# A two-layer hybrid block at full matmul occupancy: one weight sum moved to an accumulating transfer, sums and splits regrouped, two more seven-product groups

## The chip, the cores and the metric

The kernel runs on one core of one Trainium2 chip. The metric is the device time of one execution in microseconds; the median of three runs is given, with the lowest and the highest. A profile of one more execution gives its own time and, inside it, the span from the first to the last instruction.

The engines are called by the profile's names: PE (TensorE, matmuls), PEld (its weight loads), DVE (VectorE), ACT (ScalarE), POOL (GpSimd), SP (SyncE, which here only issues transfers).

## The reference

The input is one sequence of 256 rows with 2048 features in float32. Two layers are applied, and a last normalisation:

```
for layer in range(2):
    h = h + mixer(rmsnorm(h, norm[layer]))      # layer 0: gated delta rule + RG-LRU; layer 1: forgetting attention + block attention
    h = h + swiglu(rmsnorm(h, ffn_norm[layer]), w_gate, w_up, w_down)
return rmsnorm(h, final_norm)

swiglu(hn) = (silu(hn @ w_gate) * (hn @ w_up)) @ w_down      # 2048 -> 5632 -> 2048
```

Nearly all of the work is products of the 256 rows with weight matrices that are read once from memory. The two feed-forward parts (FFN, `swiglu`) take more than half of the time, and nearly all of the change lies there.

## The kernel before

**Exact products from two halves.** Every float32 matrix, weights and activations, is split into a high part in the matmul's reduced format (`hi`, a cast on ACT) and the remainder (`lo`, a subtraction on DVE). A product is three matmuls: high by high, high by low, low by high. A weight piece is 128 x 1024 (two tiles of 128 x 512, 512 KB). `load` (line 166) asks for it on SP's queue into a `raw` buffer; `split` (line 176) makes `whi` and `wlo`. One call of `Bank.add` (line 399) is one product of a piece with one half of the rows: two tiles by three matmuls of 128 x 512, six in all.

**Groups by sevens.** An FFN is cut into blocks (`block`, line 409). A gate-and-up block works out 512 columns of both the gate and the up matrix from all 2048 features; there are 11 in an FFN. Feature blocks are taken in groups of 512 features: for one group, the weights are a 2 by 2 matrix of pieces (`b11`, `b12`, `b21`, `b22`), and the rows of the activations are two halves. A plain group takes 8 products. A group by sevens (`seven`, line 424) takes 7, after Winograd's scheme: four of the seven use sums of the weight pieces, worked out on the fly, and three of them use combinations of the activations, which `combine` (line 382) works out once for a group of features and keeps in `comb`. Four of the products go to four banks `M[0]` to `M[3]` of their own, three right into the banks `F`; at the end of a block `ends` (line 449) takes the four together on ACT and DVE.

**Which groups are by sevens.** `groups` in `ffn` (line 501) gives for each of the 11 gate-and-up blocks how many of its four groups are done by sevens: none in block 0, two in every other. A piece of 4, 4 and 3 blocks is followed by two blocks of the down projection (`dn`), each with one group by sevens. That makes 26 groups by sevens per FFN.

**The sums before.** `total` (line 372) adds two pieces on DVE into a new tile `T`, and at once casts and splits the sum into `thi` and `tlo`. A group has four: T1 = `b11 + b12`, T3 = `b12 + b22`, T2 = T1 + `b22`, T4 = T2 + `b21`. The tag `T` has three buffers, which `combine` (its `cf` and `cc4`) and the scratch of the squares (`sumsq`, line 313) use as well.

**What sets the order.** The program is written in one order, and the framework's planner orders the instructions of each engine by priority in that order and by estimated times; semaphores follow from the tiles. Groups by sevens are generators of seven steps that are taken between the plain pieces: after piece `j` of a block, steps are taken up to `(j - lead + 2) * steps // gaps`, with `lead` plain pieces ahead and `trail` behind (line 475). `hooks` run before a plain piece: `turn` (the transposes of the last block's result) before piece 2, `rstd` and two `combine` in block 0, and the `combine` for the down projection (`late`) before piece 4 of one block.

**Buffers for weight pieces.** In the FFNs `load` takes three buffers of `wr` and four of `raw4`, four of each seven loads going to `raw4`; SP issues a load when the buffer is free again, so a buffer that is kept long holds up SP's queue. `whi` has four buffers, `wlo` three, `thi` and `tlo` two each.

**Start and end.** `first` (line 210) does the first four weight tiles while activations and weights come in, in 16 slices of features: four loads of one slice, then six of two; splits go by halves for the first two pairs (`u < 2`). In the LRU part of the first mixer every tile has a generator that runs beside the next tile's matmuls; `start(..., pace)` says after how many turns it takes its next step. At the end, `second_half` (line 1137) has a written order for DVE and ACT: last sums, squares, the root and reciprocal of the mean (`root`, `rate`), and the scaled outputs (`ready`).

Of the kernel before, what the change touches and what calls it, by code (L numbers as in the profile page):

```python
# [6 lines left out]
ALU = mybir.AluOpType  # L7
# [3 lines left out]
D = 2048  # L11
# [36 lines left out]
def body(tc, A, out):  # L48
# [117 lines left out]
    def load(src):  # L166

        loads[0] += 1
        if more and loads[0] > 0 and loads[0] % 7 in (1, 3, 5, 6):
            raw = mx.tile([128, 1024], F32, name="raw4", tag="raw4", bufs=4)  # L170
        else:
            raw = wr.tile([128, 1024], F32, name="raw")
        nc.sync.dma_start(raw, src)
        return raw
# [35 lines left out]
    def first(src, n, w):  # L210
# [7 lines left out]
        Ps = [acc.tile([128, T], F32, name="Pw", tag="acc") for _ in range(n)]  # L218
        for a, b in [(k, k + 1) for k in range(4)] + [(k, k + 2) for k in range(4, NK, 2)]:
            nc.sync.dma_start(xw[a // 4][:, a % 4:a % 4 + b - a], src[:, a:b])  # L220
            if b == 12:
                nc.sync.dma_start(tab[:, 0:NTAB0], A["tab"][:, 0:NTAB0])
                nc.sync.dma_start(col[:, 16:], A["col"][:, 16:])
        for u in range(NK // 2):
            hi = wh.tile([128, 1024], F32R, name="whi")
            lo = wl.tile([128, 1024], F32R, name="wlo")
            for a, b in [(0, 1), (1, 2)] if u < 2 else [(0, 2)]:
                ks = range(2 * u + a, 2 * u + b)
# [84 lines left out]
    def sumsq(g, *ts):  # L313
        for t in ts or range(2):
            j = (mx.tile([128, 1024], F32, name="junk", tag="T", bufs=3)[:, 0:512] if more else
                 mx.tile([128, 512], F32, name="junk", tag="t2", bufs=4))
            S.activation(j, h[:, t, g * 512:(g + 1) * 512], AF.Square, accum_out=ssp[:, t, g:g + 1])
# [53 lines left out]

    def total(a, b, name):

        t = mx.tile([128, 1024], F32, name=name, tag="T", bufs=3)
        V.tensor_tensor(out=t, in0=a, in1=b, op=ALU.add)  # L375
        hi = fp.tile([128, 1024], F32R, name="thi", tag="thi", bufs=2)
        lo = fp.tile([128, 1024], F32R, name="tlo", tag="tlo", bufs=2)
        S.copy(hi, t)  # L378
        V.tensor_sub(lo, t, hi.bitcast(F32))  # L379
        return t, (hi, lo)  # L380

    def combine(x4):

        f = mx.tile([128, 4, T], F32, name="cf", tag="T", bufs=3)
        c = mx.tile([128, 4, 2, 128], F32, name="cc4", tag="T", bufs=3)
        r = fp.tile([128, 2, 4, 2, 128], F32R, name="comb", tag="comb", bufs=3)
# [22 lines left out]
    def block(src, x, comb, nd, hooks, tail=0, lead=2, trail=None):  # L409
# [14 lines left out]
        def seven(m):  # L424
            c = comb[m]()
            cx = lambda i: lambda kk: [c[:, j, i, kk] for j in range(2)]
            q = lambda j, t: lambda kk: xs(4 * m + 2 * j + kk, t)
            b11 = load(src(0, 2 * m))
            M[0].add(q(0, 0), split(b11))
            yield  # L430
            b12 = load(src(1, 2 * m))
            t, w = total(b11, b12, "T1")
            M[1].add(cx(0), w)
            yield
            b22 = load(src(1, 2 * m + 1))
            F[0][1].add(cx(3), split(b22))
            yield
            M[3].add(cx(1), total(b12, b22, "T3")[1])
            yield
            t, w = total(t, b22, "T2")  # L440
            M[2].add(cx(2), w)
            yield
            b21 = load(src(0, 2 * m + 1))
            F[0][0].add(q(1, 0), split(b21))
            yield
            F[1][0].add(q(1, 1), total(t, b21, "T4")[1])
            yield
# [34 lines left out]
    def ffn(L, then, fin=None):  # L482
# [17 lines left out]

        for groups in ((0, 2, 2, 2), (2, 2, 2, 2), (2, 2, 2)):
            piece = len(groups)
            hid = ogp.tile([128, 16, 2, T], F32R, name="hid", tag="hid")
            late = {4: lambda hid=hid: ch.update({0: combine(hid[:, 0:4])})}
            for j in range(piece):
# [5 lines left out]
                if j == 1 and piece == 3:  # L511
                    hooks.update(late)
                F, e = block(lambda i, u: gu[b, u, i], lambda k: X[:, k], {m: lambda m=m: cx[m] for m in range(groups[j])}, 4, hooks)
                a = [fp.tile([128, 512], F32, name=f"fa{t}", tag="fa", bufs=2) for t in range(2)]
# [81 lines left out]
    def mixer0():  # L596
# [540 lines left out]
    def second_half(add):  # L1137

        o = fo[0]
        x, y, z = ([f[:, t:t + 1] for t in range(2)] for f in (xf, yf, zf))  # L1140

        def root(t):

            for i, o in ((2, z[t]), (3, x[t])):
                V.scalar_tensor_tensor(out=o, in0=ssp[:, t, i:i + 1], scalar=1.0 / D, in1=part[:, t:t + 1] if i == 2 else z[t],
                                       op0=ALU.mult, op1=ALU.add)
            S.activation(y[t], ssp[:, t, 3:4], AF.Sqrt, scale=1.0 / D, bias=z[t])
# [30 lines left out]
        rate(1)  # L1178
# [98 lines left out]
```

## Time and profile before

| what | value |
|---|---|
| median of 3 runs | 2233.04 us (2232.82 to 2233.43) |
| the profiled execution | 2232.51 us |
| its span, first to last instruction | 2230.7 us |
| granted PE clock | 0.999 |
| moved by transfers | 422.29 MB, mean 189 GB/s |
| first mixer, second mixer (about) | 0 to 433 us, 1101 to 1528 us |
| the two FFNs (about) | 433 to 1128 us, 1528 to 2221 us |

A row of a group names the line, the engine, the operation, output<-inputs by the program's names, the shape, the count, then the busy time, the mean time of one in ns, and the engine's idle time just before such an instruction with what ended it. A row of waits reads: who waited <- for whom: us in total, times, longest. A row of the timeline gives start and duration in us, and in brackets the idle time before it and what ended that. Matmuls overlap, so that their durations are longer than the distance between their starts.

### The profile page before, as it was taken

To read this page: it belongs to the slowest core of one execution; us is meant where nothing else is said; L and a number is where in the kernel's file an instruction comes from. 1 tells how busy PE (TensorE), PEld (TensorE's weight loads), DVE (VectorE), ACT (ScalarE), POOL (GpSimd) and SP (SyncE) were. 2 spreads that over 40 slices of the span, in tenths; PEclk is the share of its full clock that TensorE was granted. 3 is DMA by queue.
4 is the path that set the end of the run, shared out by engine and by line. 5 is a ranking of instruction groups with operands and counts; after the bars stand their busy time and mean duration, and the time that the engine had idled before them with its cause. 6 is when DMAs were issued, how large, how long until landed. Compare 5 with 4: busy or idle time off the path is not lost.

```text
span 2230.7 us, 30096 instructions
## 1 busy us (share of the span) xinstructions
PE 2215.9 (99%) x11026; PEld 1852.0 (83%) x11026; DVE 1928.9 (86%) x2716; ACT 1278.9 (57%) x1670; POOL 2.1 (0%) x6
## 2 busy tenths in 40 slices
PE   9999999999999999999999999999999999999998
PEld 8888888888888888888878888888888888888886
DVE  8899676789989999899966658857999999999998
ACT  6776664565555665565654444445665466555565
POOL 0000000000000000000000000000000000000000
PEclk9999999999999999999999999999999999999999
DMA  7445445665565666656545455456665666666563
GB/s 280 161 144 168 140 150 187 214 208 195 192 215 196 201 195 203 207 187 200 180 158 175 158 172 172 162 186 217 208 198 191 208 205 203 194 210 202 181 219 131
DMA packets 117780, 422.29 MB, mean 189 GB/s; under 512 B 13152, under 2 KB 14688, under 8 KB 117504
## 3 DMA queue, kind: packets, MB, share of 16 engines
q1 hardware_dynamic: 117344, 420.10, 56.7%
q8 instruction: 86, 1.41, 0.2%
q14 instruction: 62, 0.51, 0.1%
q10 hardware_dynamic: 288, 0.27, 0.0%
HBM read 418.22 MB, written 2.10 MB: 188 GB/s over the span
## 4 chain that ended last, share of the span: by engine, by line
PE 97%; DVE 1%; DMA 1%; ACT 0%; issue 0%; SPq 0%; DVEq 0%; ACTq 0%
PE F L405 16%; PE F L406 16%; PE F L404 16%; PE Pw L199 11%; PE Pw L204 6%; PE Px L303 5%; PE Px L305 5%; PE Px L304 5%; PE M L404 4%; PE M L405 4%; PE M L406 4%; PE Ph L492 1%; PE Psc L1053 1%; PE Pt L326 0%; PE Ps L563 0%; DMA raw<-in_gu 0%
## 5 line engine op out<-in xcount | busy, mean ns | idle before, releaser
L179 ACT CAST whi<-raw 128x1024 fp32r<-128x1024 f32 x724 | 760.7, 1052 | 744.8 <-PE F L406 359.1
L180 DVE TENSOR_TENSOR wlo<-raw,whi 128x1024 fp32r<-128x1024 f32 x724 | 876.5, 1219 | 185.0 <-PE Px L304 74.0
L199 PE MATMUL Pw<-X,whi 128*128 128x512 f32 x1088 | 388.0, 400 | 0.0
L404 PE MATMUL F<-whi,X 128*128 128x512 f32 x848 | 330.5, 391 | 0.0
L405 PE MATMUL F<-wlo,X 128*128 128x512 f32 x848 | 330.4, 390 | 0.0
L406 PE MATMUL F<-whi,X 128*128 128x512 f32 x848 | 330.1, 389 | 0.0
L204 PE MATMUL Pw<-X,wlo 128*128 128x256 f32 x1088 | 304.7, 280 | 0.1
L378 ACT CAST thi<-T 128x1024 fp32r<-128x1024 f32 x208 | 219.1, 1054 | 98.6 <-DVE T L375 71.5
L379 DVE TENSOR_TENSOR tlo<-T,thi 128x1024 fp32r<-128x1024 f32 x208 | 252.5, 1219 | 24.7 <-ACT thi L378 24.2
L199 PEld LDWEIGHTS Pw<-X,whi 128*128 128x128 f32 x1088 | 204.1, 188 | 47.4 <-issue 0.5
L405 PE MATMUL F<-wlo,hid 128*128 128x512 f32 x536 | 208.9, 390 | 0.0
L406 PE MATMUL F<-whi,hid 128*128 128x512 f32 x536 | 208.7, 389 | 0.0
L404 PE MATMUL F<-whi,hid 128*128 128x512 f32 x536 | 208.6, 390 | 0.0
L204 PEld LDWEIGHTS Pw<-X,wlo 128*128 128x128 f32 x1088 | 205.4, 189 | 1.2 <-DVE wlo L180 0.7
L406 PEld LDWEIGHTS F<-whi,X 128*128 128x128 f32 x848 | 159.2, 188 | 33.1
L404 PEld LDWEIGHTS F<-whi,X 128*128 128x128 f32 x848 | 159.2, 188 | 32.7
L405 PEld LDWEIGHTS F<-wlo,X 128*128 128x128 f32 x848 | 159.3, 188 | 32.5
L375 DVE TENSOR_TENSOR T<-raw,raw 128x1024 f32<-128x1024 f32 x98 | 119.2, 1218 | 11.0 <-DMA raw<-in_gu 8.9
L375 DVE TENSOR_TENSOR T<-T,raw 128x1024 f32<-128x1024 f32 x104 | 126.6, 1218 | 1.9 <-DMA raw<-in_dn 1.7
L404 PE MATMUL M<-thi,comb 128*128 128x512 f32 x312 | 121.3, 391 | 0.6 <-ACT thi L378 0.6
L405 PE MATMUL M<-tlo,comb 128*128 128x512 f32 x312 | 121.6, 390 | 0.0
L406 PE MATMUL M<-thi,comb 128*128 128x512 f32 x312 | 121.5, 389 | 0.0
(385 smaller groups left out, 3217.1 us busy)
## 6 DMA issues: line engine op xcount, KB each, us to landing
raw<-in_gu SPq DMA_DIRECT2D x352, 512.0 KB, 4.1
raw<-in_dn SPq DMA_DIRECT2D x176, 512.0 KB, 4.3
raw<-in_w0w SPq DMA_DIRECT2D x72, 512.0 KB, 3.6
raw<-in_wo SPq DMA_DIRECT2D x64, 512.0 KB, 3.5
raw<-in_w1w SPq DMA_DIRECT2D x64, 512.0 KB, 3.6
raw<-in_w1x SPq DMA_DIRECT2D x32, 512.0 KB, 3.6
raw<-in_w0x SPq DMA_DIRECT2D x16, 512.0 KB, 3.6
xw<-in_xw SPq DMA_DIRECT2D x6, 768.0 KB, 10.9
```

Of the source, the lines that this page charges most:

```text
L179: S.copy(hi, raw)
L180: V.tensor_sub(lo, raw, hi.bitcast(F32))
L199: PE.matmul(P.rearrange("p a b -> p (a b)"), hi[:, kk], X[:, k].rearrange("p a b -> p (a b)"), start=k == 0, stop=False)
L204: PE.matmul(P[:, 0], lo[:, kk], X[:, k, 0], start=False, stop=k == NK - 1)
L303: PE.matmul(Ps[t], x[:, 0, ts], hi[:, kk], start=k == 0, stop=False)
L304: PE.matmul(Ps[t], x[:, 0, ts], lo[:, kk], start=False, stop=False)
L375: V.tensor_tensor(out=t, in0=a, in1=b, op=ALU.add)
L378: S.copy(hi, t)
L379: V.tensor_sub(lo, t, hi.bitcast(F32))
L404: PE.matmul(self.t, xh, hi[:, kk], start=self.i == kk == 0, stop=False)
L405: PE.matmul(self.t, xh, lo[:, kk], start=False, stop=False)
L406: PE.matmul(self.t, xl, hi[:, kk], start=False, stop=kk == 1 and self.i == self.n - 1)
```

## The change

- In a group by sevens, only three sums stay on DVE. The first, `b11 + b12`, is written to `T`; the later ones are added to the same tile in place, each after the split of the one before. The sum `b12 + b22` is made by a transfer that POOL issues: it reads `b22` from memory a second time and adds it to the buffer of `b12`.
- The steps of a group are put in another order: `b12` is loaded in the first step together with `b11`, each sum is made one step ahead of its cast and split, and `b12 + b22` is split in the sixth step.
- `T` has two buffers in place of three, `raw4` five in place of four (five of each eight loads); the scratch of the squares moves to the tag `fa`.
- Block 0 of each FFN does its first group by sevens, with `lead=6`; the others keep 2, and all gate-and-up blocks a `trail` of 2. That makes 27 groups per FFN. The late `combine` in the last piece moves from before piece 4 to before piece 6.
- In `first`, six slices are loaded singly in place of four, and three pairs are split by halves in place of two. The generator of the first LRU tile has a pace of 4.
- At the end, the two additions of the mean are taken out of `root`; the first is placed ahead of the outputs that are ready, the second behind the root.

```
-        if more and loads[0] > 0 and loads[0] % 7 in (1, 3, 5, 6):
-            raw = mx.tile([128, 1024], F32, name="raw4", tag="raw4", bufs=4)
+        if more and loads[0] > 0 and loads[0] % 8 in (1, 3, 4, 6, 7):
+            raw = mx.tile([128, 1024], F32, name="raw4", tag="raw4", bufs=5)
...
-        for a, b in [(k, k + 1) for k in range(4)] + [(k, k + 2) for k in range(4, NK, 2)]:
+        for a, b in [(k, k + 1) for k in range(6)] + [(k, k + 2) for k in range(6, NK, 2)]:
...
-            for a, b in [(0, 1), (1, 2)] if u < 2 else [(0, 2)]:
+            for a, b in [(0, 1), (1, 2)] if u < 3 else [(0, 2)]:
...
-            j = (mx.tile([128, 1024], F32, name="junk", tag="T", bufs=3)[:, 0:512] if more else
+            j = (fp.tile([128, 512], F32, name="junk", tag="fa", bufs=2) if more else
...
-    def total(a, b, name):
-
-        t = mx.tile([128, 1024], F32, name=name, tag="T", bufs=3)
-        V.tensor_tensor(out=t, in0=a, in1=b, op=ALU.add)
+    def halves(t):
+
         hi = fp.tile([128, 1024], F32R, name="thi", tag="thi", bufs=2)
         lo = fp.tile([128, 1024], F32R, name="tlo", tag="tlo", bufs=2)
         S.copy(hi, t)
         V.tensor_sub(lo, t, hi.bitcast(F32))
-        return t, (hi, lo)
+        return hi, lo
...
             b11 = load(src(0, 2 * m))
             M[0].add(q(0, 0), split(b11))
-            yield
             b12 = load(src(1, 2 * m))
-            t, w = total(b11, b12, "T1")
-            M[1].add(cx(0), w)
+
+            t = mx.tile([128, 1024], F32, name="T", tag="T", bufs=2)
+            more_of = lambda a, b: V.tensor_tensor(out=t, in0=a, in1=b, op=ALU.add)
+            more_of(b11, b12)
+
+            G.dma_start(b12, src(1, 2 * m + 1), accum_op=ALU.add)
             yield
             b22 = load(src(1, 2 * m + 1))
             F[0][1].add(cx(3), split(b22))
             yield
-            M[3].add(cx(1), total(b12, b22, "T3")[1])
-            yield
-            t, w = total(t, b22, "T2")
-            M[2].add(cx(2), w)
+            M[1].add(cx(0), halves(t))
+            more_of(t, b22)
             yield
             b21 = load(src(0, 2 * m + 1))
             F[0][0].add(q(1, 0), split(b21))
             yield
-            F[1][0].add(q(1, 1), total(t, b21, "T4")[1])
+            M[2].add(cx(2), halves(t))
+            more_of(t, b21)
+            yield
+            M[3].add(cx(1), halves(b12))
+            yield
+            F[1][0].add(q(1, 1), halves(t))
             yield
...
-        for groups in ((0, 2, 2, 2), (2, 2, 2, 2), (2, 2, 2)):
+        for groups in ((1, 2, 2, 2), (2, 2, 2, 2), (2, 2, 2)):
...
-                    hooks.update(late)
-                F, e = block(..., 4, hooks)
+
+                    hooks[6] = late[4]
+                F, e = block(..., 4, hooks, lead=6 if b == 0 else 2, trail=2)
...
-            start(lru_tile(n, wstat(W[n], True), lw))
+            start(lru_tile(n, wstat(W[n], True), lw), 4 if n == 0 else 2)
...
+        def mean(t, i):
+
+            V.scalar_tensor_tensor(out=(z, x)[i][t], in0=ssp[:, t, 2 + i:3 + i], scalar=1.0 / D,
+                                   in1=z[t] if i else part[:, t:t + 1], op0=ALU.mult, op1=ALU.add)
+
         def root(t):
 
-            for i, o in ((2, z[t]), (3, x[t])):
-                V.scalar_tensor_tensor(out=o, in0=ssp[:, t, i:i + 1], scalar=1.0 / D, in1=part[:, t:t + 1] if i == 2 else z[t],
-                                       op0=ALU.mult, op1=ALU.add)
             S.activation(y[t], ssp[:, t, 3:4], AF.Sqrt, scale=1.0 / D, bias=z[t])
...
         sumsq(3, 0)
         add(1, 0)
+        mean(0, 0)
         root(0)
+        mean(0, 1)
         sumsq(2, 1)
...
         sumsq(3, 1)
+        mean(1, 0)
         ready(0, 2)
         ready(0, 3)
         root(1)
+        mean(1, 1)
         ready(0, 1)
```

More of the change, by code (lines that the diff above doesn't have):

```diff
@@ L379, in total @@
         V.tensor_sub(lo, t, hi.bitcast(F32))
-        return t, (hi, lo)
+        return hi, lo
     def combine(x4):
-        f = mx.tile([128, 4, T], F32, name="cf", tag="T", bufs=3)
-        c = mx.tile([128, 4, 2, 128], F32, name="cc4", tag="T", bufs=3)
+        f = mx.tile([128, 4, T], F32, name="cf", tag="T", bufs=2)
+        c = mx.tile([128, 4, 2, 128], F32, name="cc4", tag="T", bufs=2)
         r = fp.tile([128, 2, 4, 2, 128], F32R, name="comb", tag="comb", bufs=3)
@@ L511, in ffn @@
                 if j == 1 and piece == 3:
-                    hooks.update(late)
-                F, e = block(lambda i, u: gu[b, u, i], lambda k: X[:, k], {m: lambda m=m: cx[m] for m in range(groups[j])}, 4, hooks)
+                    hooks[6] = late[4]
+                F, e = block(lambda i, u: gu[b, u, i], lambda k: X[:, k], {m: lambda m=m: cx[m] for m in range(groups[j])}, 4, hooks, lead=6 if b == 0 else 2, trail=2)
                 a = [fp.tile([128, 512], F32, name=f"fa{t}", tag="fa", bufs=2) for t in range(2)]
```

## The prediction

> **What bounds the kernel now.** I read the page from the top: busy times, then the chain that ended last. The first line is the span of the profiled execution, the second its busy times, the third the shares of the chain.
>
> ```profile
> span 2230.7 us, 30096 instructions
> PE 2215.9 (99%) x11026; PEld 1852.0 (83%) x11026; DVE 1928.9 (86%) x2716; ACT 1278.9 (57%) x1670; POOL 2.1 (0%) x6
> PE 97%; DVE 1%; DMA 1%; ACT 0%; issue 0%; SPq 0%; DVEq 0%; ACTq 0%
> ```
>
> TensorE (PE) bounds it, at 99% busy and 97% of the chain; POOL does nothing. So work taken off DVE is worth only the time that PE now waits for DVE, and the sure gain is matmuls that go. I therefore asked next for PE's waits (its queue of matmuls alone), and for the stretch of the first feed-forward part (FFN) by itself.
>
> ```profile
> PE Pw L245 <- ACT whi L240: 0.7, 1, 0.7
> PE Pgate L645 <- ACT cx L582: 0.6, 1, 0.6
> PE M L404 <- ACT thi L378: 0.6, 1, 0.6
> PE F L405 <- DVE tlo L379: 0.4, 1, 0.4
> ...
> 440.00:1095.00 655.00, 654.60 (x2928) 540.97 (x2927) 617.48 (x646) 376.11 (x394) 0.00 (x0) 1.00 0.61 201
> ```
>
> Beside the wait at the very start, four waits of 2.3 us are all. In the FFN window (columns: PE, PEld, DVE, ACT, POOL busy, granted clock, DMA share, GB/s) DVE is busy 617 of 655 us, 94%: near PE, but behind it.
>
> What a matmul costs is its pitch, since their shown durations overlap. Two rows of the timeline, three matmuls apart:
>
> ```profile
> 2220.06 0.39 PE L406 MATMUL F<-whi,hid 128*128 128x512 f32 x1
> ...
> 2220.74 0.39 PE L406 MATMUL F<-whi,hid 128*128 128x512 f32 x1
> ```
>
> 0.68 us for three, 0.227 each; one product (six matmuls, one call of `Bank.add`) is 1.36 us.
>
> **The change, part by part.**
>
> *One group by sevens in each first block.* Block 0 of each FFN goes from 32 products (16 pieces of weight, two each) to 24 plus 7, so one product less per FFN, two in all: 2 x 1.36 = **-2.7 us**. The new group's sums and `ends` go to DVE, where block 0 had plain splits only. Its `combine` stood there before. Cover: plain pieces cost DVE one split each. `lead=6` puts the seven steps beside pieces 5 to 8, behind that `combine`.
>
> *Three sums on DVE instead of four, the fourth by POOL's accumulating transfer.* The rows of sums and splits, and the waits between them (idle time of the engine before, releaser at the end):
>
> ```profile
> L378 ACT CAST thi<-T 128x1024 fp32r<-128x1024 f32 x208 | 219.1, 1054 | 98.6 <-DVE T L375 71.5
> L379 DVE TENSOR_TENSOR tlo<-T,thi 128x1024 fp32r<-128x1024 f32 x208 | 252.5, 1219 | 24.7 <-ACT thi L378 24.2
> L375 DVE TENSOR_TENSOR T<-raw,raw 128x1024 f32<-128x1024 f32 x98 | 119.2, 1218 | 11.0 <-DMA raw<-in_gu 8.9
> ```
>
> 208 splits are 52 groups; 52 sums of 1.22 us, 63 us of DVE, leave, and the two new groups bring 2 x 10 instructions less 2 x 4 plain splits, 15 us. About 48 us of 1929 go, some 3.7% of DVE's time in the FFNs. On PE this is worth nothing by itself, as the chain says.
>
> *Sums a step ahead of splits.* Today sum, cast and subtraction follow one another: ACT idles 71.5 us for sums and DVE 24.2 us for casts. A step between them takes most of this away. PE's share of it is in two places of the timeline:
>
> ```profile
> 759.09 0.39 PE L404 MATMUL F<-thi,X 128*128 128x512 f32 x1
> ...
> 759.87 0.50 PE L405 MATMUL F<-tlo,X 128*128 128x512 f32 x1 [0.40 <-DVE tlo L379]
> ...
> 2167.03 0.39 PE L404 MATMUL F<-whi,comb 128*128 128x512 f32 x1
> ...
> 2168.02 0.50 PE L404 MATMUL M<-thi,comb 128*128 128x512 f32 x1 [0.60 <-ACT thi L378]
> ```
>
> Start to start these are 0.78 and 0.99 us where 0.227 is the pitch: 0.55 and 0.76 lost, 1.3 in all. I take **-1.2 us** (ends: 0, if others come in their place, and -5.5, if all waits of the weight loads for sums and splits were PE's own loss):
>
> ```profile
> PEld F L405 <- DVE tlo L379: 2.4, 6, 0.8
> PEld M L404 <- ACT thi L378: 2.2, 5, 1.0
> ...
> PEld F L404 <- ACT thi L378: 0.9, 4, 0.3
> ```
>
> *What the transfer needs.* It can start when the second piece, `b12`, has been read by the first sum, and must land before `b12` is split, five steps on. In a block with two groups 14 steps stand beside 4 plain pieces: 48 + 84 = 132 matmuls, 29.9 us, 2.14 us a step, so 10.7 us. No row shows an accumulating transfer or one issued by POOL. The nearest:
>
> ```profile
> raw<-in_gu SPq DMA_DIRECT2D x352, 512.0 KB, 4.1
> ...
> xw<-in_xw SPq DMA_DIRECT2D x6, 768.0 KB, 10.9
> ...
> fin<-in_fw SPq DMA_DIRECT2D x1, 1024.0 KB, 7.5
> ```
>
> It moves 512 KB in and must read what it adds to, so I take the 1024 KB row, 7.5 us; ends 4.1 (a plain load) and 10.9 (a load in a full queue). 7.5 is hidden with 3.2 us to spare; 10.9 would be 0.2 us late in a group, which the split tiles that DVE and ACT hold ready before PE cover. So **0** at both of these ends. POOL has nothing queued behind it; ACT's cast of `b12`, though, holds up every later cast on ACT, and those hold DVE and PE.
>
> Engines of the DMA: 201 GB/s at a share of 0.61 is 330 GB/s in full, 1.6 us for a 512 KB piece. 27 more pieces an FFN, each counted twice, are 86 us in some 690: the share goes from 0.61 to 0.73. Not full, but the loads on SP's queue may land later. Those are held by buffers, as SP's own waits say:
>
> ```profile
> SPq L173 <- DVE wlo L180: 1425.7, 571, 6.8
> SPq L173 <- DVE T L375: 287.6, 139, 6.4
> ```
>
> `b12` is now asked for a step earlier, right behind `b11`, and keeps its buffer three steps longer, `b11` and `b22` one less each: 2.1 us more a group, against an eighth buffer. I take **0**. (If the cover is gone: a load late costs PE what the row at 759.87 shows, 0.55 us.)
>
> *T tiles 3 to 2, the late `combine` from piece 4 to piece 6, squares' scratch from T to `fa`.* `combine` needs both T tiles, so it now waits until the groups of its block are over; its six DVE instructions, two like L375 and four of a quarter (my estimate: 3.7 us), stand before the next block's splits. The result is wanted a block later. The squares write where the transposes of piece 2 have read. **0**; if the lead is short, up to 3.7 us once an FFN.
>
> *First loads and first splits.* SP issues one DMA more before the rest (some 0.5 us of SP: four take 1.99 us in a row, below), and the third pair is split by halves.
>
> ```profile
> 2.59 1.99 SPq L220 DMA_DIRECT2D xw<-in_xw  x4
> ...
> 8.63 0.60 ACT L240 CAST whi<-h 128x512 fp32r<-128x512 f32 x1
> ...
> 9.27 1.06 ACT L250 ACTIVATE h<-h 128x1024 f32<-128x1024 f32 x1
> ...
> 10.24 0.89 ACT L231 ACTIVATE X<-xw,col 128x256 fp32r<-128x256 f32 x2
> ...
> 11.04 1.03 ACT L240 CAST whi<-xw 128x1024 fp32r<-128x1024 f32 x1
> ...
> 11.19 0.28 PE L247 MATMUL Pw<-X,wlo 128*128 128x256 f32 x1
> 12.12 0.38 PE L245 MATMUL Pw<-X,whi 128*128 128x256 f32 x1 [0.65 <-ACT whi L240]
> ```
>
> PE starts 0.8 us late at 12.12, waiting for two scalings (0.89) and a cast of 1.03. By halves it is one scaling and a cast of 0.60, from 10.3: the first matmul at about 11.4, 0.7 earlier. The next pair's subtraction is then the tight one, so I keep **-0.6** (ends: +0.5 for SP's extra issue, -0.9).
>
> *First LRU tile, pace 4 for 2.* The second wait of PE's list, 0.62 us for the `cx` and `cv` work of the gates, goes: **-0.6**, ends 0 (the next tile waits instead) and -0.8.
>
> *The end.* From the last matmul on:
>
> ```profile
> 2221.16 0.69 DVE L542 TENSOR_TENSOR h<-F,e 128x512 f32<-128x512 f32 x1 [0.16 <-PE F L406]
> 2221.77 1.41 DVE L1159 SCALAR_TENSOR_TENSOR fin<-h,fin,fin 128x512 f32<-128x512 f32 x2
> ...
> 2222.43 0.19 ACT L317 ACTIVATION_READ_ACCUMULATOR junk<-h 128x1 f32 x1
> 2223.09 0.42 DVE L1145 SCALAR_TENSOR_TENSOR fin<-ssp,fin 128x1 f32<-128x1 f32 x2
> 2223.34 0.29 ACT L1147 ACTIVATE fin<-ssp,fin 128x1 f32<-128x1 f32 x1 [0.73 <-DVE fin L1145]
> 2223.54 2.11 ACT L1157 ACTIVATE fin<-fin,fin 128x512 f32<-128x512 f32 x3
> 2223.67 0.16 DVE L1151 RECIPROCAL fin<-fin 128x1 f32<-128x1 f32 x1 [0.15 <-ACT fin L1147]
> ```
>
> With the first mean ahead of the two outputs, the root starts when the squares are read, 2222.62, not at 2223.34. DVE still does the same instructions in a row, so the reciprocal gains only its idle 0.15: **-0.15**.
>
> Sum: -2.7 - 1.2 - 0.6 - 0.6 - 0.15 = **-5.3 us**. The profiled execution took 2232.51, so 2227.2; it lies 0.5 under the median of the runs, so I say **2227.7**.
>
> **The rivals.**
>
> *Only the products go.* PE was waiting 2.3 us in four places; a new order of five engines' work may make as many new ones. Then -2.7, 2230.3, within 0.2% (4.5 us, about what a measurement of this kernel tells from no change). For it: every other term is under 1.3 us and hangs on a place. Against: DVE has more slack afterwards. Chance 0.27.
>
> *The accumulating transfer is late: slower.* Place: ACT's cast of `b12`. Point from which it decides: a landing over 10.7 us after the sum, 3.2 more than I took. For it: DVE works 94% of the FFN beside a POOL that has issued no transfer here yet, and the DMA share rises. Against: the rows up to 1024 KB lie below 10.7. Price: with PE losing 0.55 us in each of the 54 groups, as at 759.87, 30 us, and the 1.2 us stay: 2227.7 + 1.2 + 30 = 2259. Chance 0.23. The Trainium skill, "SBUF — State Buffer", section "Who interferes with whom", speaks for it in part: it says that a DMA from GpSimd waits for its descriptors while DVE holds the port pair they share, and gives 3100 ns for one of 620; but it says this of copies and one-tensor operations, and not of two-tensor sums, which DVE mostly runs here. By its figure the landing would be 7.5 + 2.5 = 10.0 us (an estimate), still hidden; no run here shows it yet.
>
> *It is a larger gain*, with most of the weight loads' 5.5 us gone too: 2224.5; part of the likeliest case.
>
> **How the numbers follow.** Likeliest, 0.50: 2227.7, own range 2224.5 to 2228.5 (below, two thirds of the way from the sum to all favourable ends together, -10 us or 2223.0; above, the 0.2% bound at 2228.6). Products only, 0.27: 2228.6 to 2232. Late transfer, 0.23: from 2234 up. The range 2224.5 to 2238 leaves out some 0.05 below and 0.15 above, the late case where PE loses over 0.2 us a group. Faster 0.50, same 0.27, slower 0.23.
>
> **What would show it.** 216 casts `thi` and 162 sums on DVE, 54 transfers on POOL's queue, landing in 5 to 10 us; PE's waits for `thi` and `tlo` gone; ACT's idle time before `thi` down from 98.6 us by half or more; DVE in the FFN window under 92%; no wait of ACT on the transfer. The first block of each FFN 1.36 us shorter. I am wrong if ACT or PE wait for `b12`, if loads land in over 6 us, or if a wait at 12 or 188 us only moves.

## The result, and the profile after

The changed kernel takes 2251.89 us (median of 5 runs, 2250.47 to 2252.91), against 2233.04 before: a ratio of 1.0081, 95% interval 1.0067 to 1.0095. It is 18 us slower by this ratio (18.9 between the two medians), where the prediction said 5 us faster. The profiled execution took 2250.47 us.

The first lines of the page after, its shares of the chain, and the FFN window that was shown of before:

```profile
span 2248.7 us, 30352 instructions
PE 2221.9 (99%) x11014; PEld 1846.0 (82%) x11014; DVE 1903.1 (85%) x2693; ACT 1281.7 (57%) x1679; POOL 48.9 (2%) x60
PE 89%; DVE 5%; DMA 3%; issue 1%; ACT 1%; DVEq 0%; SPq 0%; ACTq 0%
...
440.00:1095.00 655.00, 647.67 (x2878) 529.75 (x2877) 597.90 (x624) 372.81 (x391) 23.44 (x27) 1.00 0.73 222
```

PE has 12 matmuls less, as it should, and DVE fell from 617 to 598 us of this window, 91%. Yet PE's part of the chain fell from 97% to 89%, and transfers (3%) and DVE (5%) rose from 1% each. In the same 655 us PE got through 2878 matmuls where it was 2928: 50 x 0.227, some 11 us, lost in the first FFN alone. PE's own waits after the change (who waited <- for whom: us in total, times, longest):

```profile
PE F L403 <- DVE tlo L377: 5.3, 10, 1.2
PE F L402 <- ACT thi L376: 3.2, 3, 1.8
...
PE F L403 <- DVE wlo L180: 2.6, 4, 0.8
PE F L402 <- ACT whi L179: 1.7, 3, 1.0
PE Pgate L650 <- ACT V L837: 0.8, 1, 0.8
PE Pw L204 <- DVE wlo L180: 0.5, 1, 0.5
```

The first four are all in the FFNs: 12.8 us in 20 places, where two waits of together 1.0 us stood. A wait costs more than its idle time. Counted from the starts of the FFNs' matmuls, with all that goes over the pitch of 0.227 us as lost, PE loses 25.1 us after the change and lost 6.1 before: 19 us more, against 2.7 saved. DVE has more time than before, and yet the halves come later. No instruction got slower: in both profiles the mean is 1.05 us for a cast and 1.22 for a subtraction, and the granted clock in this window is 1.00. The rows of splits and of the loads, before's being 98.6 us of idle time ahead of 208 `thi` and 4.1 us for a load:

```profile
L376 ACT CAST thi<-T 128x1024 fp32r<-128x1024 f32 x162 | 170.3, 1053 | 103.4 <-DVE T L431 77.5
L376 ACT CAST thi<-raw 128x1024 fp32r<-128x1024 f32 x54 | 56.8, 1051 | 10.5 <-PE M L404 7.8 <-ACT whi L179 2.7
...
raw<-in_gu SPq DMA_DIRECT2D x352, 512.0 KB, 4.5
raw<-in_gu POOLq DMA_DIRECT2D x42, 512.0 KB, 8.1
```

The sum made by the transfer is split from `raw`, in the second row, so that 113.9 us of idle time stand ahead of 216 casts. How one of the losses comes about: the chain that ended last between 694 and 709 us, then the timeline there.

```profile
697.06 8.79 DMA raw<-in_gu
...
706.90 1.05 ACT thi L376
...
707.99 0.72 PE F L402 x2
```

```profile
696.43 0.86 POOL L434 DMA_DIRECT2D raw<-in_gu  x1 [20.62 <-ACT whi L179]
...
705.95 1.04 ACT L179 CAST whi<-raw 128x1024 fp32r<-128x1024 f32 x1 [2.79 <-DMA raw<-in_gu]
706.90 1.99 ACT L376 CAST thi<-T 128x1024 fp32r<-128x1024 f32 x2
```

POOL's accumulating transfer goes out at 696.43. SP's plain load, issued at 697.06 beside it, takes 8.79 us where 4.1 was usual. ACT idles 2.79 us on this load, with a sum that is ready next in its order; the cast of the sum comes late, and PE waits for `thi`. The transfer itself is late for nobody: its landings are 5.2 to 9.6 us, all under 10.7, each lies before the cast that reads it, and no wait of ACT on it shows. That it is the transfer that makes the plain load late, and not this place in the order, e1 shows below.

A second kind of loss has no transfer in it. Between 722 and 726 us, where the last steps of a group stand:

```profile
722.06 1.06 ACT L376 CAST thi<-T 128x1024 fp32r<-128x1024 f32 x1 [0.30 <-PE M L404]
...
723.02 0.68 DVE L457 TENSOR_TENSOR e<-M,e 128x512 f32<-128x512 f32 x1
...
723.46 1.05 ACT L376 CAST thi<-T 128x1024 fp32r<-128x1024 f32 x1 [0.35 <-PE M L404]
723.62 1.21 DVE L377 TENSOR_TENSOR tlo<-T,thi 128x1024 fp32r<-128x1024 f32 x1
...
724.89 0.50 PE L403 MATMUL F<-tlo,X 128*128 128x512 f32 x1 [0.31 <-DVE tlo L377]
...
725.35 1.21 DVE L377 TENSOR_TENSOR tlo<-T,thi 128x1024 fp32r<-128x1024 f32 x1
```

Each cast waits for a matmul that still reads one of the two buffers of `thi`. A split takes 1.05 on ACT and 1.21 on DVE, 2.26 us in a row; with two buffers, only the one product between, 1.36 us of PE, covers it. In the new order the last three products of a group (steps 5, 6 and 7) all use sums; in the old order a plain product lay between them. Casts waited so before the change as well (23.6 of the 98.6 us ahead of `thi`), and the short cover is not the whole of it. Here DVE first does an operation of `ends` (723.02, 0.68 us), so that the split that began at 722.06 is over at 724.83 and not at about 724.3 (my estimate, 722.06 + 2.26), which PE would not have waited for. It is so in all ten of PE's waits for `tlo`: one operation of `ends` stands just ahead of the subtraction, and in nine of them the subtraction starts 0.46 to 1.13 us after its cast has ended.

### The profile page after: what moved, and what is told of

Its sections match the earlier page's. It is cut to its first block, busy times and chain, and to the rows that moved or that the text cites. A ratio compares the mean times of both kernels' runs of the same rounds, so it can differ in the third digit from the quotient of the medians.

```text
span 2248.7 us, 30352 instructions
## 1 busy us (share of the span) xinstructions
PE 2221.9 (99%) x11014; PEld 1846.0 (82%) x11014; DVE 1903.1 (85%) x2693; ACT 1281.7 (57%) x1679; POOL 48.9 (2%) x60
## 4 chain that ended last, share of the span: by engine, by line
PE 89%; DVE 5%; DMA 3%; issue 1%; ACT 1%; DVEq 0%; SPq 0%; ACTq 0%
PE F L403 15%; PE F L404 14%; PE F L402 14%; PE Pw L199 10%; PE Pw L204 5%; PE Px L303 5%; PE Px L304 5%; PE Px L305 5%; PE M L403 4%; PE M L402 4%; PE M L404 3%; DMA raw<-in_gu 3%; DVE wlo L180 2%; DVE tlo L377 1%; PE Ph L496 1%
## 5 line engine op out<-in xcount | busy, mean ns | idle before, releaser
L402 PE MATMUL F<-whi,X 128*128 128x512 f32 x820 | 321.1, 392 | 1.5 <-ACT whi L179 1.5
L403 PE MATMUL F<-wlo,X 128*128 128x512 f32 x820 | 319.9, 390 | 1.5 <-DVE wlo L180 1.5
L404 PE MATMUL F<-whi,X 128*128 128x512 f32 x820 | 319.7, 390 | 0.0
L376 ACT CAST thi<-T 128x1024 fp32r<-128x1024 f32 x162 | 170.3, 1053 | 103.4 <-DVE T L431 77.5
L377 DVE TENSOR_TENSOR tlo<-T,thi 128x1024 fp32r<-128x1024 f32 x162 | 197.0, 1218 | 24.6 <-ACT thi L376 23.4
L403 PEld LDWEIGHTS F<-wlo,X 128*128 128x128 f32 x820 | 154.0, 188 | 34.0 <-DVE wlo L180 2.1
L402 PEld LDWEIGHTS F<-whi,X 128*128 128x128 f32 x820 | 154.0, 188 | 32.4 <-ACT whi L179 2.3
L404 PEld LDWEIGHTS F<-whi,X 128*128 128x128 f32 x820 | 153.9, 188 | 32.4
L431 DVE TENSOR_TENSOR T<-T,raw 128x1024 f32<-128x1024 f32 x108 | 131.6, 1219 | 1.9 <-DMA raw<-in_gu 1.2
L404 PE MATMUL M<-thi,comb 128*128 128x512 f32 x324 | 126.1, 389 | 0.0
L402 PE MATMUL M<-thi,comb 128*128 128x512 f32 x324 | 126.0, 389 | 0.0
L404 PEld LDWEIGHTS F<-whi,hid 128*128 128x128 f32 x536 | 100.6, 188 | 20.9
```

Source lines behind the costliest of these rows:

```text
L402: PE.matmul(self.t, xh, hi[:, kk], start=self.i == kk == 0, stop=False)
L403: PE.matmul(self.t, xh, lo[:, kk], start=False, stop=False)
L404: PE.matmul(self.t, xl, hi[:, kk], start=False, stop=kk == 1 and self.i == self.n - 1)
L431: more_of = lambda a, b: V.tensor_tensor(out=t, in0=a, in1=b, op=ALU.add)
```

## The experiments

Two theories stood at the start. A: the accumulating transfer costs the time, by slowing the loads beside it. B: the new order of the steps costs it, by three splits of sums in a row against two buffers. A rival to A: `b12` is held too long, or its landing is waited for. Open beside these was what became of the products saved. Ratios are against the kernel before on the same chip, with 95% intervals.

**e1: the sum on DVE again, in place, in the new order.**

```
-            G.dma_start(b12, src(1, 2 * m + 1), accum_op=ALU.add)
...
+            V.tensor_tensor(out=b12, in0=b12, in1=b22, op=ALU.add)
```

> The changed kernel with the transfer taken away: b12 + b22 is added on DVE in place, behind the second sum of its group; step order, buffers, first-block group, start and end stay as changed. Theory A (the accumulating transfer and the plain loads beside it slow one another: loads beside it took 5.6 us on the mean, others 4.3): the loads land in 4.2 us again, the waits of PE in the FFNs fall from about 25 us to 6 plus what the first blocks lose (some 5), so about 2237 us, against 2251.9 with the transfer. Theory B (the new order of steps: three splits of sums in steps 5, 6 and 7 against two buffers of thi and tlo): the waits before tlo in the last step stay, 2248 to 2254 us.

2240.63 us, 1.0028 (1.0018 to 1.0037), nearer to theory A's 2237 than to theory B's 2248. The transfer is worth 0.53%, some 12 us: the larger part. With DVE back at 626 us of the window the kernel is faster, so DVE's relief bought nothing. e1 issues the same 528 loads of the FFNs in the same order as the change, so the two can be compared load by load, from issue to landing. The 209 that overlap a transfer in the change take 5.5 us in the mean there and 4.5 in e1, and 60 of them take over 6 us where in e1 3 do; the 319 others take 4.3 in both. The median of the page hides this: 4.5 for `in_gu` in the change, 4.4 in e1, where theory A said 4.2. Counted from the starts of the matmuls, PE's loss in the FFNs falls from 25.1 us to 12.9. Some 6 us stay lost without any transfer, and `tlo` is waited for still:

```profile
PE F L403 <- DVE wlo L180: 1.9, 2, 1.0
PE F L403 <- DVE tlo L377: 1.8, 6, 0.4
```

On DVE, an operation of `ends` (4 places) or the next group's first sum (4) stands ahead of the late subtraction in the eight places where PE loses most on `tlo`.

**e2: POOL's transfer made plain.** Nothing is added, so that one of the four sums is left out; reads, order and buffers are those of the change.

```
-            G.dma_start(b12, src(1, 2 * m + 1), accum_op=ALU.add)
+            G.dma_start(b12, src(1, 2 * m + 1))
```

> The changed kernel with the transfer on POOL's queue left as a plain load of the same 512 KB over b12 (the sum b12 + b22 is left out, so the result is not the reference's). If it is the added traffic and the second queue that slow the loads, it stays within 3 us of 2251.9 and loads beside it still take over 5 us. If it is the accumulation itself, that reads its destination too, the transfer lands in about 4 to 5 us, loads beside it in 4.5, and the time falls most of the way to that of the kernel with the sum on DVE, to about 2240 us. Theory B: 2248 to 2254 us with the transfer landing early.

2246.21 us, 1.0055 (1.0039 to 1.0072): halfway, which none of the three expectations was. About half of the price is there for a plain 512 KB transfer at this place, the rest for the adding.

**e3: the change without the group in block 0.**

```
-        for groups in ((1, 2, 2, 2), (2, 2, 2, 2), (2, 2, 2)):
+        for groups in ((0, 2, 2, 2), (2, 2, 2, 2), (2, 2, 2)):
...
-                F, e = block(..., 4, hooks, lead=6 if b == 0 else 2, trail=2)
+                F, e = block(..., 4, hooks, lead=2, trail=2)
```

> The changed kernel with no group by sevens in block 0 (groups 0, lead 2), all else as changed. Two products more cost 2.7 us. Theory C (the first block's group stands behind combine and rstd on DVE and the loads fall behind, 2.7 and 3.1 us of PE waits at 452 and 1557 us): the net is -2.8 us, about 2249 us. If block 0 costs nothing but its products: 2254.6 us.

2250.85 us, 1.0078 (1.0063 to 1.0093): not to be told from the change, so the group in block 0 neither explains the 18 us nor brings a gain that the runs can see. The profile says why: the 4.3 us that PE waits for `whi` and `wlo` in the FFNs of the change all lie in the two first blocks, and are gone here.

**e4: before, with the first loads and splits, the LRU pace and the order of the end alone.**

```
-        for a, b in [(k, k + 1) for k in range(4)] + [(k, k + 2) for k in range(4, NK, 2)]:
+        for a, b in [(k, k + 1) for k in range(6)] + [(k, k + 2) for k in range(6, NK, 2)]:
...
-            start(lru_tile(n, wstat(W[n], True), lw))
+            start(lru_tile(n, wstat(W[n], True), lw), 4 if n == 0 else 2)
```

> The kernel before with only the new first loads and splits, the pace of the first LRU tile, and the new order at the end. My terms were -0.6, -0.6 and -0.15: 2231.7 us. By the changed kernel's profile the start gives 0.9 and the end 0.35, but the LRU wait has only moved (0.8 us at 195 us) and new waits stand at 74 and 118 us: about 2232.8 us, no change that can be told.

2233.28 us, 0.9997 (0.9987 to 1.0006): too small to be told from nothing.

**e5: e1 with the old step order.**

```
             more_of(b11, b12)
+            yield
+            M[1].add(cx(0), halves(t))
             yield
...
             F[0][1].add(cx(3), split(b22))
-            yield
-            M[1].add(cx(0), halves(t))
-            more_of(t, b22)
             V.tensor_tensor(out=b12, in0=b12, in1=b22, op=ALU.add)
+            more_of(t, b22)
             yield
-            b21 = load(src(0, 2 * m + 1))
-            F[0][0].add(q(1, 0), split(b21))
+            M[3].add(cx(1), halves(b12))
             yield
             M[2].add(cx(2), halves(t))
-            more_of(t, b21)
             yield
-            M[3].add(cx(1), halves(b12))
+            b21 = load(src(0, 2 * m + 1))
+            F[0][0].add(q(1, 0), split(b21))
+            more_of(t, b21)
             yield
```

> The kernel with the sum on DVE (no transfer), and its seven steps put back in the order of before: the split of T1 in step 2, of b12 + b22 in step 4, of T2 in step 5, of T4 in step 7, sums still in place and ahead of the splits. Theory B (splits of sums in steps 5, 6 and 7 against two buffers of thi and tlo make PE wait for the last one): PE's waits for thi and tlo in the FFNs, with the short ones about 6 us, go; from 1.0028 of before it falls to 1.000 to 0.999. If the order is not it: it stays at 1.002 to 1.004.

2231.62 us, 0.9989 (0.9980 to 0.9998): faster than before, if barely, and 0.39%, some 9 us, faster than e1 by the order alone, in which `b12` is also free two steps earlier. PE's waits for `thi` and `tlo` are gone, and its loss counted from the starts is 6.1 us, as before; of waits, this is what is left in the FFNs:

```profile
PE F L403 <- DVE wlo L180: 0.7, 2, 0.6
```

**e6: before with the group in block 0.**

```
-        for groups in ((0, 2, 2, 2), (2, 2, 2, 2), (2, 2, 2)):
+        for groups in ((1, 2, 2, 2), (2, 2, 2, 2), (2, 2, 2)):
...
-                F, e = block(..., 4, hooks)
+                F, e = block(..., 4, hooks, lead=6 if b == 0 else 2, trail=2)
```

> The kernel before with one group by sevens in block 0 of each FFN (lead 6, trail 2), nothing else. My term: two products less, -2.7 us, ratio 0.9988. Theory C (the group stands behind combine, rstd and ends on DVE in block 0, where the changed kernels lose 1.0 to 3.1 us a block): the gain is eaten, ratio 0.9995 to 1.001.

2236.97 us, 1.0014 (1.0005 to 1.0022): 3 us slower where the products alone would give 2.7 faster. PE's waits, then the chain in block 0 (a part of it):

```profile
PE F L405 <- DVE wlo L180: 4.0, 4, 1.7
```

```profile
441.66 5.71 DMA raw<-in_gu
...
447.39 1.24 DVE T L375
448.63 0.02 SPq L173
...
448.68 3.59 DMA raw<-in_gu
...
452.30 0.04 DVE T L375
```

In block 0 the chain runs through loads: the first sum waits for one (5.71 us), the next load goes out from SP only when that sum has ended, and the second sum waits for it in turn (3.59 us). PE's 4.0 us of waiting are more than the 2.7 saved.

**e7: the transfer only in the 12 groups of the down projections**, the other 42 sums on DVE as in e1.

```
-            G.dma_start(b12, src(1, 2 * m + 1), accum_op=ALU.add)
+            if down:
+                G.dma_start(b12, src(1, 2 * m + 1), accum_op=ALU.add)
```

> The changed kernel with the transfer in the 12 down-projection groups alone (the 42 gate-and-up groups add on DVE). Theory A, by dose: 12 of 54 of the transfer's 11 us would be 2.5 us over the kernel with all sums on DVE, ratio about 1.004. Theory A, by place (loads that land late are felt where two groups stand beside 4 plain pieces; in the changed kernel no wait over 0.1 us lies on a product of hid): nothing, ratio 1.002 to 1.003.

2242.32 us, 1.0034 (1.0021 to 1.0047): 0.06% above e1 for 12 of 54 transfers, where an even share of e1's 0.53% would be 0.12%. The interval holds both, and zero.

**e8: e5 with block 0's work moved.** The first `combine` comes before piece 3, `rstd` before piece 10, the second `combine` in block 1, and the LRU pace is that of before.

```
-                    hooks[5] = lambda: cx.update({0: combine(X[:, 0:4])})
-                    hooks[8] = rstd
-                    hooks[10] = lambda: cx.update({1: combine(X[:, 4:8])})
+                    hooks[3] = lambda: cx.update({0: combine(X[:, 0:4])})
+                    hooks[10] = rstd
+                if b == 1:
+                    hooks[0] = lambda: cx.update({1: combine(X[:, 4:8])})
```

> The kernel with the old step order and the sum on DVE, and block 0 relieved: its own combine before piece 3 in place of 5, rstd before piece 10 in place of 8, the second combine in the block after; the LRU pace as before. Theory C (the group in block 0 waits for a split that stands behind combine and rstd on DVE): the 1.0 us of waits for wlo in the two blocks go, and the 0.8 us at the gates stays about as it was; 0.998 to 0.999, about 2 us under before or a little more. If block 0 loses for another reason: no change from 0.9989.

2231.52 us, 0.9993 (0.9984 to 1.0002): as e5, and not the 0.998 to 0.999 of theory C. The waits for `wlo` did not go either: they are 3.0 us in three places where e5 had 0.7. Moving these hooks does not relieve block 0.

**e9 and e10: a third order, without and with the transfer.** Sums are split in steps 2, 4, 6 and 7, so two in a row at most, and `b12` is held to step 6. e9 adds `b22` to `b12` on DVE; e10 has the accumulating transfer and is else the same.

```
             more_of(b11, b12)
+            yield
+            M[1].add(cx(0), halves(t))
             yield
...
-            yield
-            M[1].add(cx(0), halves(t))
             more_of(t, b22)
...
             yield
+            M[2].add(cx(2), halves(t))
+            yield
             b21 = load(src(0, 2 * m + 1))
             F[0][0].add(q(1, 0), split(b21))
-            yield
-            M[2].add(cx(2), halves(t))
             more_of(t, b21)
```

> No transfer, sum on DVE; splits of sums in steps 2, 4, 6 and 7, so two in a row at most, but b12 keeps its buffer until step 6, as in the changed kernel. Theory B (three splits in a row against two buffers of thi and tlo): near the kernel with the old order (0.9989), 0.998 to 1.000. Rival B' (b12's long hold keeps SP from loading in time): near the kernel with three in a row (1.0028), 1.002 to 1.004.

> The same order (2, 4, 6, 7) with the accumulating transfer of the changed kernel. If the transfer costs by itself what it cost in the changed order (11 us over the sum on DVE, 0.5%): 1.003 to 1.005. If it was felt only because three splits in a row had used up the lead of DVE and ACT: within 0.15% of the same order with the sum on DVE, about 0.999 to 1.0005.

e9: 2233.28 us, 1.0000 (0.9991 to 1.0009). e10: 2246.80, 1.0056 (1.0044 to 1.0069). This order, in which `b12` is held as long as in the change, lies 0.28% under e1 and 0.11% over e5: most of what the change's order costs goes with the three splits in a row, and the hold with the rest is worth about 0.1%, which the intervals do not tell from nothing. How much of it is the short cover, and how much DVE's other work ahead of a subtraction, no run separates. The transfer costs 0.56% again, 13 us: its price does not hang on the three splits in a row. In e10, unlike in the change, ACT also waits three times for a landing of the transfer itself:

```profile
ACT thi L376 <- DMA raw<-in_gu: 5.0, 3, 2.0
```

**e11 and e13: a transfer that nobody waits for.** Both are e5 with four buffers `raw4` of seven loads, as before; e11 adds in every group a transfer of the same size and kind into a tile that nobody reads. The tile is cleared once an FFN; a one-column copy by POOL starts each transfer.

```
+            G.tensor_copy(out=side[0][:, 0:1], in_=t[:, 0:1])
+            G.dma_start(side[0], src(1, 2 * m + 1), accum_op=ALU.add)
```

> The old step order with in-place sums on DVE and four raw4 buffers, and beside it, in every group, an accumulating transfer by POOL into a tile of its own that nobody reads (a one-column copy on POOL after the first sum starts it). Nothing waits for this transfer and it holds no piece of weight. Theory A (the transfer's price is what it does to the plain loads beside it): 8 to 13 us above the same kernel without it, ratio 1.003 to 1.005, waits of PE for thi and tlo back, loads on SP's queue from 4.2 to 4.5 us or more. Rival (the price is the hold of b12 and the cast that waits for it): within 2 us of the kernel without it.

> The old step order with in-place sums on DVE, and four raw4 buffers of seven loads as before in place of five of eight: the kernel that the run with the side transfer is to be compared with. Theory A: b12 is not held long in this order, so the fifth buffer is worth nothing, 0.9985 to 0.9995, as with five (0.9989). Rival (the fifth buffer carries the gain of that version): over 1.0005, SP's loads later.

e13: 2233.35 us, 1.0001 (0.9993 to 1.0010); e11: 2255.90, 1.0103 (1.0087 to 1.0119). Twice what theory A said, 22.6 us; and the timeline shows a second cause in e11, of my own making:

```profile
1669.85 4.52 POOL L438 COPY side<-T 128x1 f32<-128x1 f32 x1 [20.97 <-DVE T L433]
1670.84 1.22 DVE L445 TENSOR_TENSOR raw<-raw,raw 128x1024 f32<-128x1024 f32 x1
...
1674.41 1.23 DVE L433 TENSOR_TENSOR T<-T,raw 128x1024 f32<-128x1024 f32 x1
```

POOL's copy of one column takes 4.52 us beside DVE's sums, and the next sum into `T` starts 0.04 us after it ends. So e11 mixes two causes.

**e14 and e15: the same with the copy on DVE (0.145 us), and with a plain transfer.** In e15 nothing is added.

```
-            G.tensor_copy(out=side[0][:, 0:1], in_=t[:, 0:1])
+            V.tensor_copy(out=side[0][:, 0:1], in_=t[:, 0:1])
             G.dma_start(side[0], src(1, 2 * m + 1), accum_op=ALU.add)    # e15: without accum_op
```

> As the run with the side transfer, but the one-column copy that starts the transfer is on DVE, not on POOL, where it took up to 4.5 us and kept the tile T from its next sum. Theory A (the transfer slows the plain loads beside it): still 8 to 15 us above the same kernel without it (2233.35), ratio 1.0035 to 1.007, PE's waits for thi and tlo back, ends of idle time of ACT on raw<-in_gu. Rival (POOL's copy made those 22 us): within 3 us, at most 1.0014.

> The same with a plain side transfer: 512 KB read from memory and written, nothing added. Theory A in halves (half is mere traffic on a second queue, half the accumulation, as the earlier plain transfer said): 4 to 7 us above 2233.35, ratio 1.002 to 1.003, and loads beside it at 5.1 us or so. Rival B (it is the accumulation alone): within 2 us. Rival C (it is the second queue alone): as much as with the accumulation.

e14: 2241.61 us, 1.0034 (1.0022 to 1.0047); e15: 2237.89, 1.0017 (1.0008 to 1.0026), each just under the lower end of theory A's range. Over e13's 2233.35 a plain side transfer costs 4.5 us and an accumulating one 8.3 (by ratio, since e13 ran on another chip, 3.6 and 7.4), though no product waits for either and no piece of weight is held. The 54 small copies on DVE are in both, and their share is not measured. That is the half-and-half of e2 again, without the rival's cause: theory A holds for 7 to 8 of the 12 to 13 us. PE's waits in the FFNs go from 1.5 us in e13 to 7.7 in e14, 5.6 of them for `whi` and `wlo`, the halves of plain loads. What the other 4 or 5 are is open: `b12` held for the transfer, or loads hit harder where POOL's transfer stands in the change. Landing times of e14 and of e15, in this order, and e13's plain load:

```profile
side<-in_gu POOLq DMA_DIRECT2D x42, 512.0 KB, 6.4
```

```profile
side<-in_gu POOLq DMA_DIRECT2D x42, 512.0 KB, 4.7
```

```profile
raw<-in_gu SPq DMA_DIRECT2D x352, 512.0 KB, 4.1
```

In e14 and e15 the median of SP's loads is 4.4. Load by load against e13, whose order of loads is the same, those that overlap a transfer take 4.8 us in the mean where they took 4.1 (e14), and 4.4 where they took 3.9 (e15).

**e12: e5 without the group in block 0.** Two lines go back, as in e3.

> The old step order with in-place sums on DVE, five raw4 buffers, and block 0 of each FFN without its group. Theory A (in this order the group keeps about half of its 2.7 us, the profile of the version with it shows 1.4 us of losses in the two blocks): 0.9992 to 0.9998 against 0.9989 with it, PE without the waits for wlo at about 454 and 1549 us. Rival (the group is worth nothing here either): 0.9984 to 0.9990.

2230.59 us, 0.9988 (0.9980 to 0.9997): the rival was right, the group is worth nothing that can be told in the good order either. The profile has 12 matmuls more than e5, 2.7 us, and counted from the starts PE loses 3.8 us in the FFNs where e5 loses 6.1, so that 2.3 of the 2.7 are eaten. PE waits for nothing there; beside the wait at the very start, its longest are these:

```profile
PE Pgate L649 <- ACT V L836: 0.8, 1, 0.8
PE Pw L245 <- ACT X L231: 0.2, 1, 0.2
PE Pss L722 <- ACT kt L754: 0.2, 1, 0.2
```

e12 and e5 beat the kernel before by 0.1%; between the two no run can tell.

## Why the prediction was wrong

By ratio the 0.81% is made up so: the transfer +0.53% (e1 to the change), the order of the steps +0.39% (e5 to e1), all the rest -0.11% (before to e5): 11.8 + 8.7 - 2.5 = 18.0 us.

**What the transfer needs, "I take 0": the step that failed, by 12 us.** The landing time was well estimated (7.5, the median 8.1 for `in_gu`), and the bar of 10.7 us was not reached (the cast of its sum follows the transfer's issue by 7.6 us at least and 19.6 in the median, and every transfer had landed by then), so the rival in the form I gave it, a late landing, did not happen either, though it had the right sign: by luck, since its cause did not occur. I asked whether the transfer would land in time for its own reader, and priced its effect on others with the mean share of the DMA engines (0.61 to 0.73, which came true: 0.73). The mean hides what one load sees. Of SP's loads for the FFNs, the 209 that overlap one of the transfers take 5.5 us in the mean and up to 9.2, where the same loads take 4.5 without the transfers (e1). I wrote that "a load late costs PE what the row at 759.87 shows, 0.55 us", if the cover is gone, and then kept 0. The row at 705.95 shows what no buffer covers: behind the cast that waits for a late load stands, in ACT's order, the sum that PE needs next. The Trainium skill, "DMA: Bandwidth & Descriptors", section "Issuing engines are not separate DMA queues", says that transfers of all issuing engines run on the same 16 engines and interleave. e15 agrees: beside a plain transfer on POOL's queue SP's loads take 4.4 us where 3.9 was the mean. Of the 12 us of this term, 7 to 8 are shown to be such loads made late (e14); the other 4 or 5 stay open.

**Sums a step ahead of splits, -1.2: wrong, +8.7.** I looked at what a step of distance does for one sum and its cast, and not at what the new order puts side by side. ACT's idle time before `thi` did not fall by half but rose from 98.6 to 113.9 us. It was no good sign to go by: e5, which is faster, has 112.8. The lower end of my range for this, "0, if others come in their place", was named for the wrong reason: the place is three products from sums in a row, a split of 2.26 us against a cover of 1.36, with DVE at work for `ends` or the next sum between cast and subtraction. The two numbers stood in my own rows. e5 shows that the sums in place, each added a step or more ahead of its split, are harmless when the old order of products is kept.

**Products, -2.7: counted right, and worth nothing that can be told.** The 12 matmuls are gone from the page. In the kernel before the group costs 3 us (e6), in the change it brings nothing that can be told (e3), and with the order put back nothing either (e12). "Plain pieces cost DVE one split each" was true but not the question: in block 0 the sums wait for their loads (e6's chain). Which of block 0's loads or small operations would have to come earlier is open; moving e8's hooks did not do it.

**DVE relief worth 0: right.** DVE stands at 91% of the window, under the 92% I gave, and e1, with all sums on DVE, is faster.

**Buffers: 0, off by a little.** With the order of e5, the fifth `raw4` buffer is worth 0.12% (e13's 1.0001 to 0.9989), about as much as can be told; my expectation for e13, that it is worth nothing there, missed by little. `T` with two tiles, the late `combine` and the squares' scratch are in e5 too and cost nothing visible.

**First loads -0.6, LRU pace -0.6, end -0.15: -1.35 said, -0.8 us measured (e4), which the interval does not tell from none.** In the trace, the wait of 0.7 us for `whi` at 12 us is gone; PE's list has instead 0.4 us for a scaling at 5 us, and the 0.5 us for `wlo` shown above, at 74 us. The LRU wait only moved, to the next tile, and grew from 0.6 to 0.8: "the next tile waits instead" was the end of the range, and the truth. The matmul that then waits starts at 196.56 us, where the same tile's stood at 196.17 before, so up to there the profile shows no gain. The end did better than said. Its rows after (compare those from 2221.16 on):

```profile
2239.52 0.69 DVE L547 TENSOR_TENSOR h<-F,e 128x512 f32<-128x512 f32 x1 [0.92 <-PE F L404]
...
2241.77 0.16 DVE L1158 RECIPROCAL fin<-fin 128x1 f32<-128x1 f32 x1
```

```profile
2241.00 0.29 ACT L1154 ACTIVATE fin<-ssp,fin 128x1 f32<-128x1 f32 x1
```

The root follows the squares without its 0.73 us of idle time. From the last sum's start to the reciprocal it is 2.25 us where it was 2.51, and to the end of the span 9.2 where it was 9.5.

**What was to show it.** 54 transfers, 5 to 10 us, DVE under 92%, no wait on the transfer: all came. `thi` and `tlo` waits gone, ACT's idle time halved, and first blocks 1.36 us shorter: none came, for PE loses 2.7 and 3.1 us in the two first blocks, counted from the starts. Two of the conditions for being wrong were met: loads over 6 us (68 of the FFNs' 528, 7 before), and a wait that only moves.

## What to carry to other kernels

A transfer that is itself in time can still cost: ask how late the load beside it may be, and what stands behind that load's reader on an engine that works in order. A mean share of the DMA engines does not answer this. When steps are regrouped, hold the split's own time (cast and subtraction, 2.26 us) against the work that its buffers leave between two uses (1.36 us), for each neighbour pair in the new order, and see what else the engine of the subtraction has to do in between. And relief for an engine that is not the bound is no ground to pay with transfers.

## What was not expected of the hardware

- An accumulating transfer of 512 KB lands in 6.4 us where a plain one from the same place takes 4.7 (e14 and e15), and its issue holds POOL 0.86 us against 0.53. Each of 54 costs some 0.15 us (8.3 / 54; an estimate, 0.14 by ratio) without a product waiting for it.
- POOL's copy of one column takes 0.18 to 4.52 us beside DVE's sums:

```profile
L438 POOL COPY side<-T x54: 183/1114/4524, 448.3 to 2211.3; 128x1 f32<-128x1 f32 x54
```

On DVE the same copy takes 0.145 us, and the kernel 2241.61 (1.0034) in place of 2255.90 (1.0103). The Trainium skill, "SBUF — State Buffer", section "Who interferes with whom", has the rule: a DVE instruction with two inputs from SBUF contends with a GpSimd instruction that reads SBUF; these sums have two, and the trace agrees: beside them the copy took up to 4.52 us. The starving of descriptors that my rival drew from the same page (the 3100 ns stand there in the section "A bandwidth-pool intuition that's wrong (but worth ruling out)") did not show: in the change POOL's transfer instructions took 0.86 us nearly every time and 1.01 at most, and none landed over 9.6.
